# Two sets of transposes moved later, the pooling maps spread over four gate products, and a quarter of the weight splits given to ScalarE and VectorE

## The chip, the cores and the metric

The kernel runs on one core of one Trainium2 chip. The metric is the time on the device in microseconds (us), from launch to end; smaller is better. The kernel before has a median of 3289.72 us over three runs (3289.57 to 3299.82 us).

Engines in the text: TensorE (PE) multiplies, VectorE (DVE), ScalarE (ACT) and GpSimd (POOL) work on tiles in SBUF, PE writes into banks of PSUM, and SyncE (SP) and ACT issue most DMAs. Each engine executes its instructions in program order, so that an instruction that waits holds up all that stands behind it on its engine.

## The reference, cut to what matters

One layer of a streaming encoder on 2048 tokens of 1024 channels, all in float32. The part that the change touches is the input projection and what hangs on it:

```
proj = x @ w_in
q, c_kv, q_idx, w_idx, k_idx, pool_in, gate_logits = split(proj)
q     = rope(q)                                  # 8 heads of 128, first quarter rotated
k_lat = rope(c_kv);  k_idx = rope(k_idx);  q_idx = rope(q_idx)
attn  = sparse_indexed_attention(q, k_lat, c_kv, q_idx, w_idx, k_idx)   # top 256 keys of each query
pooled = trailing_mean(pool_in, windows 2/4/8/16) - pool_in
branch_b = (pooled @ w_pool per channel group * pool_scale) @ w_pool_branch
gate_a, gate_b = split(sigmoid(gate_logits))
mixed = (gate_a * branch_a + gate_b * branch_b) @ w_out
```

After it come two layer norms and a gated FFN with a short convolution, which the change leaves alone.

## The kernel before, in words

**Number format.** Products must keep float32 accuracy. Each operand is split into a high part, rounded to the matmul's input type, and the rest (`split`, line 312); each product is three matmuls (hi x hi, hi x lo, lo x hi; `mm3`). A product in the text, unless said otherwise, is 24 matmuls of 128x512 with a [128, 512] bank of PSUM as its sum. The split of a weight tile (128x1024) costs two operations in one of two ways: on POOL, in pieces of 256 columns (four pairs of TENSOR_SCALAR for the high part and TENSOR_TENSOR for the rest, printed as "x2" where two follow each other), or on ACT (an ACTIVATE for the high part) and DVE (a TENSOR_TENSOR for the rest). While the flag `self.shared` is set, which is until attention begins, weights asked for with `pool=True` go to POOL. Weights that are used by all four groups of tokens are split once, in group 0, written to DRAM and reloaded by the later groups.

**Stages.** The index projection comes first, for the four groups of 512 tokens. Then, for each group g: `proj_pool` (line 690, two weight chunks; in chunk 0 the two sums grow side by side in steps of one pair of channel blocks, so that i counts the steps in the loop of `run` at line 1866), `proj_q` (four chunks of 24 matmuls of 128x256 for each of four row blocks) and `proj_gates` (line 767). The latter has a first loop over j = 0 to 3 with two gate-a products each, here called p1 to p8, and a second loop with two gate-b products and two products of the pooling branch each. Attention follows (from about 1095 us), then the output projection and the FFN.

**Transposes.** Rotated keys and rotated query rows are [token, channel] and have to be turned by PE (128x128 transposes against `ident`). `keys` (line 631) does it for a group's keys, eight transposes into two banks that ACT and DVE copy out. For the last group, g = 3, it is the closure `done`, called at step i == 1 of `proj_pool(0)`. `store_q` (line 676) turns one chunk of query rows: twice four transposes, each followed by an ACT copy into an M buffer (a pool of eight) and a DMA from ACT's queue. `proj_q` keeps two chunks back; they are turned in `proj_gates` at j = 0 and j = 1.

**Pooling maps.** `pool_map` (line 752) multiplies each of the four pooled groups (p<-b,wpool, three matmuls each) and scales the result with ACT and DVE into two parts. It runs all four in a row at the start of j == 3, that is between p6 and p7.

**Banks.** `p1` has four one-bank tiles, given out in turn: a product can start when the tile handed out four requests earlier has been read. The sigmoid that reads a gate product is issued DG = 2 turns after the product.

**The background.** The sparse attention's top-k search for the first groups' queries runs in the background (`self.bg`, from `turn`): for each bit of a threshold, ACT counts with Sign (ACTIVATE m<-b,F) and DVE with TENSOR_SCALAR_CACHE_REDUCE (m<-b,F), and three small DVE operations decide (g, h, F). A step is put in when a model of the engines' clocks allows it, so its instructions stand in ACT's and DVE's program order between those of the projections.

Of the kernel before, what the change touches and what calls it, by code (L numbers as in the profile page):

```python
# [9 lines left out]
F32 = mybir.dt.float32  # L10
F32R = mybir.dt.float32r
# [3 lines left out]
AF = mybir.ActivationFunctionType  # L15
OP = mybir.AluOpType
# [3 lines left out]
P = 128  # L20
NB = S // P
G = 512
# [71 lines left out]
            1: ((0, 0, OP.add), (1, 1, OP.add)), 3: ((0, 1, OP.add), (1, 1, OP.add)), 6: ((1, 1, OP.add),),  # L94
            5: ((0, 1, OP.add), (0, 0, OP.subtract)), 7: ((0, 0, OP.add),)}
LASTK = 6
SCAN = 1.04
PIECE = 256

# [20 lines left out]
class Paced:  # L120
# [5 lines left out]
    def __getattr__(self, name):  # L126
# [4 lines left out]
        def call(*args, **kw):  # L131
# [4 lines left out]
            else:  # L136
# [10 lines left out]
                if name == "tensor_tensor_scan":  # L147
                    rate = SCAN
                now = max(getattr(self._c, self._w), self._c.pe)
# [110 lines left out]
class Kern:  # L260
    def __init__(self, ctx, tc, a, out):
        self.clocks = Clocks()
        self.tc, self.nc, self.a, self.out = tc, PacedCore(tc.nc, self.clocks), a, out
        self.stores, self.older, self.bg, self.late = [], [], [], []
        self.const = ctx.enter_context(tc.tile_pool(name="const", bufs=1))
        self.big = ctx.enter_context(tc.tile_pool(name="big", bufs=42))
        self.mid = ctx.enter_context(tc.tile_pool(name="mid", bufs=8))
        self.sm = ctx.enter_context(tc.tile_pool(name="sm", bufs=4))
        self.early_pool = tc.alloc_tile_pool(name="early", bufs=1)
        self.late_pool = None  # L270
        self.p1 = ctx.enter_context(tc.tile_pool(name="p1", bufs=4, space=PSUM))
        self.p2 = ctx.enter_context(tc.tile_pool(name="p2", bufs=2, space=PSUM))
        self.dram = ctx.enter_context(tc.tile_pool(name="dram", bufs=1, space=bass.MemoryType.DRAM))
        self.n, self.shared = 0, True
        self.credit = self.seen = 0.0

    def _name(self, s):
# [34 lines left out]
    def split(self, hi, lo, src, pool=False):  # L312

        nc = self.nc
        if pool:
            m = PIECE if self.shared else src.shape[1]  # L320
            if self.shared and len(src.shape) == 3:
                k = src.shape[2]
                m = max(1, PIECE // k)
            for i in range(0, src.shape[1], m):
                c = slice(i, i + m)
                nc.gpsimd.tensor_scalar(hi[:, c], src[:, c], 1.0, 1.0, op0=OP.mult, op1=OP.mult)
                nc.gpsimd.tensor_tensor(lo[:, c], src[:, c], hi[:, c].bitcast(F32), op=OP.subtract)
        else:
            nc.scalar.activation(hi, src, AF.Copy)
            nc.vector.tensor_tensor(lo, src, hi.bitcast(F32), op=OP.subtract)  # L330
# [418 lines left out]
        if self.lazy:  # L749
            self.lazy.pop(0)()  # L750

    def pool_map(self, g):
        nc = self.nc
        self.pm = []
        for k in range(4):
            t = self.pooled[k]
            ps = self.PS1()
            self.mm3(ps, self.wpool[:, 0, k], self.wpool[:, 1, k], t[:, 0], t[:, 1], True, True)
            o = self.T([P, 2, G], F32R)
            sc = self.pscale[:, k:k + 1]  # L760
            nc.scalar.activation(o[:, 0], ps, AF.Identity, scale=sc)
            nc.vector.scalar_tensor_tensor(o[:, 1], ps, sc, o[:, 0].bitcast(F32), op0=OP.mult, op1=OP.subtract)
            self.pm.append(o)
            yield 0.7

    def proj_gates(self, g):
        nc = self.nc
        base = g * self.nab + 6
        for j in range(4):
            w = self.ab.get(base + j)  # L770
            if j == 3:
                yield from self.pool_map(g)
            if self.qpend and j < 2:
                self.store_q()
            while self.lazy or j and self.fins:
                self.lazy_step()
            for i in range(2):
                ps = self.PS1()
                yield from self.proj_t(ps, w, i * P)

                def gate(dst=self.d_gm[g][:, 2 * j + i, 0], ps=ps):
                    ga = self.M([P, G])
                    nc.scalar.activation(ga, ps, AF.Sigmoid)
                    nc.scalar.dma_start(dst, ga)

                self.after(DG, gate)
                yield 5.2
        for j in range(4):
            w = self.ab.get(base + 4 + 2 * j)
            if j == 2:  # L790
                if g + 1 < NG:
                    self.load_parts(g + 1, range(NPRE))
                else:
                    self.attn_load()
            if j == 3 and g + 1 == NG:
                self.attn_setup()
                self.load_q(0)
                self.attention_start()
            gates = []
            for i in range(2):  # L800
                ps = self.PS1()
                yield from self.proj_t(ps, w, i * P)

                def gate(ps=ps):
                    gb = self.M([P, G])
                    nc.scalar.activation(gb, ps, AF.Sigmoid)
                    gates.append(gb)

                self.after(DG, gate)
                yield 5.2  # L810
            if j == 3 and g + 1 < NG:
                self.load_parts(g + 1, range(NPRE, DC // 2))
            if j == 3 and g + 1 == NG:
                self.scores_to(1)
            (wh, wl), = self.ab.get(base + 5 + 2 * j)
            for i in range(2):
                ps = self.PS1()
                c0 = i * P
                for k in range(4):
                    self.mm3(ps, wh[:, k, c0:c0 + P], wl[:, k, c0:c0 + P], self.pm[k][:, 0], self.pm[k][:, 1],  # L820
                             k == 0, k == 3)
                    if k in FW:
                        yield FINE
                self.flush()
                nc.vector.tensor_tensor(gates[i], ps, gates[i], op=OP.mult)
                self.store(self.d_gm[g][:, 2 * j + i, 1], gates[i])
                if j == 3 and g + 1 == NG:
                    self.scores_to(2 * i + 2)
                yield 2.6
# [851 lines left out]
    def down_half(self, hf):  # L1681
# [34 lines left out]
        for mi, m in enumerate(DOWN):  # L1716
# [5 lines left out]
            final = hf == 1 and mi == len(DOWN) - 1  # L1722
            lastk = LASTK if final else 2 if hf == 0 and mi == 4 else 3 if hf == 0 and mi == 5 else 0
            held = []
# [114 lines left out]
    def run(self):  # L1839
        self.qpend, self.rows, self.wi_parts, self.keyed, self.selected = [], {}, [], -1, 1  # L1840
        self.early, self.xr, self.xraw = {}, {}, {}
        self.qraw, self.qs, self.unit, self.avq, self.tails = {}, {}, {}, [], []
        self.pair, self.spill = {}, []
        self.load_x(0, range(1))
        self.posi = self.M([NB, P], I32)
        self.nc.sync.dma_start(self.posi, self.a["positions"].rearrange("o (b p) -> (o b) p", p=P))
        self.psc = self.M([4, P])
        self.nc.sync.dma_start(self.psc, self.a["pool_scale"].rearrange("o (g p) -> (o g) p", p=P))
        self.setup()
        self.wi.raw[0] = [self.wi.load_one(0, 0)]  # L1850
        self.load_x(0, range(1, 2))
        self.wi.raw[0].append(self.wi.load_one(0, 1))
        self.load_x(0, range(2, DC // 2))
        self.split_ahead(0, 1)
        self.wi.split(0)
        self.split_ahead(0, 1)
        for groups in GROUPS:
            self.bg.append((lambda g=groups[-1]: self.keyed >= g, self.scores_and_selection(groups)))
        done = None
        for g in range(NG):  # L1860
            self.run_to_end(self.proj_index(g, done))
            while self.spill:
                self.store(*self.spill.pop(0))
            done = self.finish_index(g)
        self.load_parts(0, range(NFIRST, DC // 2))
        for g in range(NG):
            for i, step in enumerate(self.proj_pool(g)):
                if i == 1 and g == 0:
                    done()
                    self.wi_parts = None  # L1870
                self.turn(step)
            self.run_to_end(self.proj_q(g))
            self.run_to_end(self.proj_gates(g))
        self.shared = False
        self.run_to_end(self.attention())
        self.settle()
        self.run_to_end(self.mix_out())
        self.settle()
        self.run_to_end(self.ffn())
        self.settle()  # L1880
        self.late_pool.release()
# [30 lines left out]
```

## Time and profile before

| | us |
|---|---|
| median of three runs | 3289.72 |
| the profiled execution | 3292.94 |
| its span, first to last instruction | 3291.2 |
| mean granted TensorE clock | 0.982 of full speed |
| PE busy | 3157.8 (96%) |
| DVE / ACT / POOL busy | 2417.7 / 1559.4 / 1279.9 |
| PE busy between 195 and 360 us | 131.5 of 165 |
| PE busy between 360 and 437 us | 75.6 of 77 |
| PE busy between 437 and 1095 us | 648.9 of 658 |

A row of the timeline gives the start, the duration, the engine, the operation, the tiles (output <- inputs, with buffer numbers left out), how often it follows itself, and in brackets the idle time ahead of it with what ended it. Nearly all operations are recorded under line 153, the wrapper that issues them, so they are told apart by tiles and shapes. A row of the windows gives the busy time of each engine in a stretch (with the count of instructions), the granted TensorE clock, the DMA share and GB/s. PE's busy rows in the stage from 195 to 360 us are the projections of group 0.

### The profile page before, as it was taken

What the parts mean: (1) busy time and instruction counts of PE and PEld (TensorE: products, weight loads), DVE (VectorE), ACT (ScalarE), POOL (GpSimd) and SP (SyncE); (2) the same over time, 40 slices, a digit from 0 to 9 for tenths busy, and PEclk for the clock granted to TensorE, in tenths of its full rate; (3) what the DMA queues carried; (4) which work ended last, traced back from release to release, by engine and by line L of the source; (5) the groups of instructions that cost most, each with busy time, mean ns of one, the idle gap of its engine ahead of it and who ended that gap; (6) DMA issues with size and microseconds to landing.
All of it is one profiled execution on the core that took longest, in us unless ns stands there. A gap on an engine that the chain in (4) does not pass through costs nothing. (4 is left out here: it accounts for less than half of the span.)

```text
span 3291.2 us, 46503 instructions
## 1 busy us (share of the span) xinstructions
PE 3157.8 (96%) x15918; PEld 2654.2 (81%) x15918; DVE 2417.7 (73%) x4271; ACT 1559.4 (47%) x2656; POOL 1279.9 (39%) x1314
## 2 busy tenths in 40 slices
PE   8988899999999899999999999999999999999998
PEld 8877688898898788788878877777778778888787
DVE  5588859986988777777766666666688865555797
ACT  3466537846777466666621133333343433222443
POOL 3139411020010688766641143443166511121673
PEclk9999899999999899999999999999999999999999
DMA  8457565653665444434464459899797665566984
GB/s 327 148 199 275 191 251 195 246 203 136 227 226 194 144 172 172 157 130 161 157 224 147 156 186 320 309 327 339 288 380 264 208 252 224 224 238 246 364 296 163
DMA packets 325675, 745.68 MB, mean 227 GB/s; under 512 B 30074, under 2 KB 115006, under 8 KB 325438
## 3 DMA queue, kind: packets, MB, share of 16 engines
q1 hardware_dynamic: 315646, 724.88, 61.5%
q10 hardware_dynamic: 9792, 17.83, 1.4%
q8 instruction: 126, 2.06, 0.3%
q14 instruction: 111, 0.91, 0.1%
HBM read 514.36 MB, written 228.23 MB: 226 GB/s over the span
## 5 line engine op out<-in xcount | busy, mean ns | idle before, releaser
L153 PE MATMUL p<-b,b 128*128 128x512 f32 (+3 forms) x12644 | 2783.7, 369 | 56.1 <-ACT b L153 24.4
L153 PEld LDWEIGHTS p<-b,b 128*128 128x128 f32 x12644 | 2175.7, 191 | 453.0 <-ACT b L153 25.0
L153 ACT ACTIVATE b<-p 128x512 fp32r<-128x512 f32 (+9 forms) x726 | 427.7, 612 | 653.6 <-PE p L153 627.0
L153 ACT ACTIVATE b<-b 128x1024 fp32r<-128x1024 f32 (+2 forms) x248 | 253.6, 1028 | 390.7 <-POOL b L153 136.4
L153 DVE TENSOR_TENSOR b<-b,b 128x1024 fp32r<-128x1024 f32 (+6 forms) x246 | 369.6, 1541 | 42.6 <-ACT b L153 39.8
L153 ACT ACTIVATE m<-b,F 128x1024 bf16<-128x1024 f32 (+3 forms) x352 | 345.8, 985 | 68.0 <-DVE F L153 43.8
L153 DVE TENSOR_SCALAR_CACHE_REDUCE m<-b,F 128x768 bf16<-128x768 f32 (+4 forms) x374 | 346.8, 949 | 11.8 <-DMA q<-m 9.9
L153 POOL TENSOR_TENSOR b<-b,b 128x256 fp32r<-128x256 f32 (+3 forms) x276 | 314.1, 1152 | 101.7 <-ACT b L153 84.9
L153 DVE TENSOR_TENSOR m<-m,p 128x512 f32<-128x512 f32 x176 | 120.3, 684 | 242.8 <-ACT b L153 182.6
L153 POOL TENSOR_TENSOR m<-b,b 128x512 f32<-128x512 f32 x99 | 140.2, 1425 | 337.4 <-issue 258.6
L153 DVE SCALAR_TENSOR_TENSOR b<-b,cw,b 128x1023 f32<-128x1023 f32 (+1 forms) x176 | 245.0, 1392 | 26.2 <-ACT b L153 25.1
L153 DVE TENSOR_TENSOR b<-p,b 128x512 fp32r<-128x512 f32 (+1 forms) x286 | 201.7, 714 | 72.3 <-ACT b L153 69.7
L153 POOL TENSOR_SCALAR b<-b 128x256 fp32r<-128x256 f32 (+3 forms) x216 | 125.8, 596 | 325.6 <-DMA b<-in_w_in_dram 122.8
L153 PE MATMUL p<-b 128*128 128x512 f32 x616 | 235.1, 393 | 5.8 <-ACT b L153 4.0
L153 POOL TENSOR_TENSOR b<-b,m 128x512 f32<-128x512 f32 x110 | 192.0, 1760 | 123.8 <-DMA m<-in_w_ffn_down_dram 74.0
L153 PE MATMUL p<-ident,b 128*128 128x128 f32 x1456 | 213.1, 274 | 24.8 <-ACT b L153 13.5
L153 DVE CUSTOM_DVE_ANT_0 b<-p,b 128x1024 f32<-128x1024 f32 (+7 forms) x192 | 174.2, 909 | 65.8 <-PE p L153 64.5
L153 PEld LDWEIGHTS p<-ident,b 128*128 128x128 f32 x1456 | 174.2, 141 | 58.7 <-ACT b L153 16.5
L153 ACT ACTIVATE b<-b,mx 128x1024 f32<-128x1024 f32 (+7 forms) x192 | 171.5, 896 | 69.7 <-DVE mx L153 63.7
L153 ACT ACTIVATE m<-p 128x512 f32<-128x512 f32 (+1 forms) x180 | 104.9, 594 | 193.6 <-PE p L153 178.9
L153 DVE SCALAR_TENSOR_TENSOR b<-b,ws,b 128x768 f32<-128x768 f32 (+5 forms) x154 | 159.8, 1065 | 40.6 <-ACT b L153 38.6
L153 PE MATMUL p<-kst,b 128*128 128x384 f32 (+3 forms) x656 | 150.6, 359 | 4.1 <-ACT b L153 2.6
(130 smaller groups left out, 2360.8 us busy)
## 6 DMA issues: line engine op xcount, KB each, us to landing
b<-uw SPq DMA_DIRECT2D x308, 512.0 KB, 6.5
b<-wp SPq DMA_DIRECT2D x192, 512.0 KB, 5.8
uw<-l SPq DMA_DIRECT2D x98, 512.0 KB, 3.0
b<-in_w_ffn_down_dram SPq DMA_DIRECT2D x154, 256.0 KB, 5.3
b<-h SPq DMA_DIRECT2D x154, 256.0 KB, 5.3
wp<-b SPq DMA_DIRECT2D x64, 512.0 KB, 5.2
uw<-b SPq DMA_DIRECT2D x56, 512.0 KB, 3.5
h<-m SPq DMA_DIRECT2D x110, 256.0 KB, 5.9
```

The lines of the kernel that those rows point to most:

```text
L153: return f(*args, **kw)
```

## The change

Four edits:

1. `done`, the key transposes of the last group, is called at step 5 instead of step 1 of `proj_pool(0)`, after the sums of chunk 0 instead of between their parts.
2. The two chunks of query rows that are left over are turned at j = 1 and 2 of the gates instead of j = 0 and 1, in all four groups.
3. `pool_map` makes one map a call. The maps come after the products p4, p5, p6 and p7 instead of all four between p6 and p7. Each of these products now yields twice (2.6 and 2.6) instead of once (5.2), and the four yields of the old `pool_map` are gone, so the number of turns is the same. The same lines in the second loop never apply, as 9 + 2j + i is over 7.
4. `split` counts its calls; while `self.shared` is set, every fourth call that asks for POOL goes to ACT and DVE instead.

```diff
 LASTK = 6
+KEYS_AT = 5
+PM_AT = (4, 5, 6, 7)
...
     def split(self, hi, lo, src, pool=False):
         nc = self.nc
-        if pool:
+        self.turns += 1
+        if pool and (not self.shared or self.turns % 4):
             m = PIECE if self.shared else src.shape[1]
...
-    def pool_map(self, g):
+    def pool_map(self, k):
         nc = self.nc
-        self.pm = []
-        for k in range(4):
-            t = self.pooled[k]
-            ...
-            self.pm.append(o)
-            yield 0.7
+        t = self.pooled[k]
+        ...
+        self.pm.append(o)
...
     def proj_gates(self, g):
+        self.pm = []
         for j in range(4):
             w = self.ab.get(base + j)
-            if j == 3:
-                yield from self.pool_map(g)
-            if self.qpend and j < 2:
+            if self.qpend and 1 <= j < 3:
                 self.store_q()
...
                 self.after(DG, gate)
-                yield 5.2
+                if 2 * j + i + 1 in PM_AT:
+                    yield 2.6
+                    self.pool_map(len(self.pm))
+                yield 2.6
...
             for i, step in enumerate(self.proj_pool(g)):
-                if i == 1 and g == 0:
+                if i == KEYS_AT and g == 0:
                     done()
```

In the order of the instructions it looks so. On PE in `proj_pool(0)` before, the eight key transposes (out of the two M tiles that the rope fills) stand between two steps of chunk 0's sums p_699 and p_700:

```order
L153 MATMUL p_700_2898<-b_2854,b_2190 128x512
L153 MATMUL p_700_2898<-b_2853,b_2191 128x512
L153 MATMUL p_701_2923<-ident_84,m_2763 128x128
L153 MATMUL p_702_2924<-ident_84,m_2764 128x128
...
L153 MATMUL p_699_2897<-b_2857,b_2200 128x512
L153 MATMUL p_699_2897<-b_2858,b_2200 128x512
```

After, at the same place of PE's program, they stand behind the end of both sums, ahead of chunk 1's first product p_736:

```order
L155 MATMUL p_700_2886<-b_2856,b_2200 128x512
L155 MATMUL p_700_2886<-b_2855,b_2201 128x512
L155 MATMUL p_722_2991<-ident_84,m_2757 128x128
L155 MATMUL p_723_2992<-ident_84,m_2758 128x128
...
L155 MATMUL p_736_3036<-b_2204,b_2867 128x512
L155 MATMUL p_736_3036<-b_2205,b_2867 128x512
```

The 24 matmuls that close the two sums have moved ahead of the transposes; the next product's weight b_2867 and b_2868 is one of those that ACT and DVE split now.

On PE in the gates of group 0 before, p6 ends (p_1140), the four maps follow, and p7 (p_1184) begins:

```order
L153 MATMUL p_1140_4540<-b_2861,b_4299 128x512
L153 MATMUL p_1168_4631<-b_3338,wpool_586 128x512 x3
L153 MATMUL p_1171_4641<-b_3516,wpool_586 128x512 x3
L153 MATMUL p_1178_4662<-b_3745,wpool_586 128x512 x3
L153 MATMUL p_1180_4669<-b_4032,wpool_586 128x512 x3
L153 MATMUL p_1184_4681<-b_2210,b_4459 128x512
```

After, p4 ends (p_1086), and the first map, the second left-over chunk's two sets of transposes and p5 (p_1127) follow; the other maps stand behind p5, p6 and p7:

```order
L155 MATMUL p_1086_4334<-b_2855,b_4091 128x512
L155 MATMUL p_1105_4399<-b_3320,wpool_586 128x512 x3
L155 MATMUL p_1123_4441<-ident_84,b_3870 128x128 x4
L155 MATMUL p_1125_4449<-ident_84,b_3870 128x128 x4
L155 MATMUL p_1127_4457<-b_2204,b_4237 128x512
```

With four banks in turn, p5's bank is that of p4, so p5 now stands behind p4's sigmoid. Before, four requests ahead of p5 lay a transposed set of query rows.

On ACT in the same group after, among the gate-b products, the high part b_5112 of a gate-b weight is made between Sign counts and the followers of the search's end (tn is its threshold); before, POOL made it:

```order
L155 ACTIVATE m_5020,wa_2711<-b_2419,F_4977 128x896
L155 ACTIVATE b_5075<-b_2282,tn_5064 128x768
L155 ACTIVATE m_5058<-p_1294_4997 128x512
L155 ACTIVATE b_5112<-b_4979 128x1024
L155 ACTIVATE b_5144<-b_2573,tn_5064 128x1024
```

On DVE the rest, b_5113, stands behind what follows that threshold (the masks b_5076 and b_5077, with the scan as SCALAR_TENSOR_TENSOR b<-b):

```order
L155 TENSOR_SCALAR tn_5064<-t_5063 128x2
L155 TENSOR_SCALAR b_5076<-b_5075 128x768
L155 SCALAR_TENSOR_TENSOR b_5077<-b_5076 128x768
...
L155 TENSOR_TENSOR b_5075<-b_5075,b_5076 128x768
L155 TENSOR_SCALAR b_5108<-b_5075 128x768
L155 TENSOR_TENSOR b_5113<-b_4979,b_5112 128x1024
```

So this weight is now made in the order of the search. In all, eleven tiles change over: POOL's order has 1079 rows instead of 1123, DVE's and ACT's have eleven more each. One is a weight of `proj_pool` ahead of the stage, eight lie in group 0, and two (the value up-projection and one query tile) at the start of attention.

More of the change, by code (lines that the diff above doesn't have):

```diff
@@ L273, in __init__ @@
         self.dram = ctx.enter_context(tc.tile_pool(name="dram", bufs=1, space=bass.MemoryType.DRAM))
-        self.n, self.shared = 0, True
+        self.n, self.shared, self.turns = 0, True, 0
         self.credit = self.seen = 0.0
@@ L750, in lazy_step @@
             self.lazy.pop(0)()
-    def pool_map(self, g):
+    def pool_map(self, k):
         nc = self.nc
-        self.pm = []
-        for k in range(4):
-            t = self.pooled[k]
[L757 to L762, printed above, removed]
-            self.pm.append(o)
-            yield 0.7
+        t = self.pooled[k]
+        ps = self.PS1()
+        self.mm3(ps, self.wpool[:, 0, k], self.wpool[:, 1, k], t[:, 0], t[:, 1], True, True)
+        o = self.T([P, 2, G], F32R)
+        sc = self.pscale[:, k:k + 1]
+        nc.scalar.activation(o[:, 0], ps, AF.Identity, scale=sc)
+        nc.vector.scalar_tensor_tensor(o[:, 1], ps, sc, o[:, 0].bitcast(F32), op0=OP.mult, op1=OP.subtract)
+        self.pm.append(o)
     def proj_gates(self, g):
@@ L809, in proj_gates @@
                 self.after(DG, gate)
-                yield 5.2
+                if 9 + 2 * j + i in PM_AT:
+                    yield 2.6
+                    self.pool_map(len(self.pm))
+                yield 2.6
             if j == 3 and g + 1 < NG:
```

## The prediction

> **What bounds the kernel now.** I read the busy times of a few stretches first, then PE's waits in the one stretch where PE is not full, and then the timelines there. Columns of the first row: length, busy time of PE, its weight loads, DVE, ACT and POOL, then the clock.
>
> ```profile
> 195.00:360.00 165.00, 131.51 (x723) 113.44 (x722) 150.33 (x409) 105.84 (x215) 118.81 (x216) 0.87 0.72 252
> PE p L153 <- ACT m L153: 10.6, 4, 5.1
> PE p L153 <- DVE m L153: 10.2, 6, 4.0
> PE p L153 <- ACT b L153: 9.3, 4, 3.5
> PE p L153 <- DVE b L153: 3.4, 1, 3.4
> ```
>
> PE lacks 33.5 us here, and the four rows (total, times, longest) add up to that. Elsewhere PE leads; only here, where DVE is busy 150 of 165 us, can an edit to order pay. The places:
>
> ```profile
> 208.75 0.48 PE L153 MATMUL p<-ident,m 128*128 128x128 f32 x1 [3.98 <-DVE m L153]
> ...
> 214.91 47.26 PE L153 MATMUL p<-b,b 128*128 128x512 f32 x312
> ...
> 310.39 22.05 PE L153 MATMUL p<-b,b 128*128 128x512 f32 x96 [0.74 <-ACT m L153]
> 332.27 0.87 PE L153 MATMUL p<-b,wpool 128*128 128x512 f32 x3
> ...
> 345.60 1.65 PE L153 MATMUL p<-b,wpool 128*128 128x512 f32 x3 [5.13 <-ACT m L153]
> 350.62 9.70 PE L153 MATMUL p<-b,b 128*128 128x512 f32 x33 [3.38 <-DVE b L153]
> 359.71 74.73 PE L153 MATMUL p<-b,b 128*128 128x512 f32 x329
> ```
>
> The keys' transposes (p<-ident,m) wait 10.2 us for the rope's last copies on DVE. The maps wait for sigmoids on ACT, and p7 for the first map's eviction on DVE. A warm matmul is 74.73 / 329 = 0.227 us, a product of 24 is 5.45. From p6's end at 332.27 to p7 at 350.62 are 18.35 us, of which four maps at full clock are 12 x 0.227 = 2.7; so 15.6 us are lost, and more behind them, because the clock falls:
>
> ```profile
> 345.00:350.00 5.00, 1.65 (x3) 0.83 (x3) 4.83 (x9) 1.86 (x5) 3.80 (x7) 0.50 0.53 150
> 350.00:355.00 5.00, 4.38 (x11) 3.50 (x12) 4.93 (x14) 3.48 (x8) 0.00 (x0) 0.52 1.02 396
> ```
>
> With a clock of 0.52 until 355, p7's first 4.4 us do half their work: 4.38 x 0.48 = 2.1 us lost.
>
> What do ACT and DVE hold? ACT stands about 12 us behind PE: p4 is the second product of the row at 310.39 and ends near 310.39 + 10.9 = 321.3, its sigmoid runs here:
>
> ```profile
> 333.72 0.57 ACT L153 ACTIVATE m<-p 128x512 f32<-128x512 f32 x1
> ...
> 324.09 5.29 DVE L153 SCALAR_TENSOR_TENSOR g<-wd,wa 128x4 f32<-128x4 f32 x1
> ...
> 332.30 0.16 DVE L153 SCALAR_TENSOR_TENSOR g<-wd,wa 128x4 f32<-128x4 f32 x1
> ...
> 345.27 3.56 DVE L153 SCALAR_TENSOR_TENSOR g<-wd,wa 128x4 f32<-128x4 f32 x1
> ```
>
> The lag is the search's: ACT's counts wait for DVE's decisions, and the same four-column decision takes 0.16 us or, beside POOL, 3.56 and 5.29.
>
> **What POOL costs DVE, and what a tile moved is worth.** The four commonest decisions from 195 to 360 us, POOL's split pieces there, and the split on DVE and ACT before 195 us, where it has no POOL beside it for the most part:
>
> ```profile
> L153 DVE SCALAR_TENSOR_TENSOR g<-wd,wa 128x4 f32<-128x4 f32 x26 | 15.7, 605 | 4.6 <-ACT m L153 3.9
> L153 DVE TENSOR_SCALAR h<-g 128x4 int32<-128x4 f32 x26 | 9.8, 378 | 0.8
> L153 DVE TENSOR_SCALAR h<-g 128x2 int32<-128x2 f32 x27 | 9.4, 347 | 0.9
> L153 DVE SCALAR_TENSOR_TENSOR g<-wd,wa 128x2 f32<-128x2 f32 x27 | 8.9, 330 | 0.4
> ...
> L153 POOL TENSOR_TENSOR b<-b,b 128x256 fp32r<-128x256 f32 x96 | 70.4, 755 | 0.0
> L153 POOL TENSOR_SCALAR b<-b 128x256 fp32r<-128x256 f32 x94 | 38.1, 423 | 6.7 <-DMA b<-in_w_in_dram 6.7
> ...
> L153 DVE TENSOR_TENSOR b<-b,b 128x1024 fp32r<-128x1024 f32 x17 | 20.8, 1243 | 12.8 <-ACT b L153 12.3 <-DMA xT<-b 0.3
> ...
> L153 ACT ACTIVATE b<-b 128x1024 fp32r<-128x1024 f32 x17 | 17.5, 1053 | 8.8 <-DMA b<-in_xT_dram 6.6 <-DMA b<-in_w_in_dram 2.2
> ...
> L153 DVE TENSOR_TENSOR b<-b,b 128x1024 fp32r<-128x1024 f32 x142 | 238.5, 1719 | 36.3 <-ACT b L153 34.5 <-DMA x<-b 0.9 <-DMA xT<-b 0.3
> ```
>
> 96 pieces are 24 tiles, (70.4 + 38.1) / 24 = 4.5 us of POOL each. The 106 decisions take 43.8 us where 106 x 0.16 would be 17.0: 26.8 us extra, or 1.1 us of DVE a tile. The rope's and other small operations suffer too, so I put a removed tile at 1.1 to 2.0 us of DVE. On the bill stand 1.24 us on DVE (1.72 if the mean of the whole kernel holds, the last row) and 1.05 us on ACT. The net for DVE lies between +0.6 and -0.8 us; I take -0.4, nearer the relief, since the operations counted are only part of those that suffer. Four such tiles lie ahead of p4's sigmoid: -1.6 us.
>
> The Trainium skill, "SBUF — State Buffer", on the port pair that DVE and GpSimd share, speaks against this edit: a DVE operation with two SBUF inputs, and the split's rest is one, and a GpSimd operation that reads SBUF lock each other out for a whole instruction. By it the moved split would be held up by one POOL piece, about 0.7 us, and each tile would end near -0.4 + 0.7 = +0.3 us, +1.2 in place of -1.6. The trace agrees in direction but not in the length of the hold: 5.29 us is seven pieces.
>
> **Keys' transposes.** They come 24 matmuls later, 5.45 us of PE. The end of the rope is the condition:
>
> ```profile
> 205.47 0.76 DVE L153 TENSOR_TENSOR rope<-b,sin 128x72 f32<-128x72 f32 x1
> ...
> 213.83 0.23 DVE L153 TENSOR_TENSOR rope<-b,sin 128x72 f32<-128x72 f32 x1
> ...
> 214.50 0.23 DVE L153 COPY m<-b 128x128 f32<-128x128 f32 x1
> ...
> 211.09 1.40 POOL L153 TENSOR_TENSOR b<-b,b 128x256 fp32r<-128x256 f32 x2
> ```
>
> The last copy ends at 214.73. PE would be at the transposes near 202 + 5.45 = 207.5, so they still wait, 3 to 10 us. Rope operations take 0.76 beside POOL and 0.23 once POOL stops at 212.5. In the new order two of POOL's tiles stand behind the copies of chunk 0's sums and wait for them, which frees the rope; three or four us of search that DVE did later now stand inside the rope. I put the last copy at 211 to 218. PE then has 24 matmuls done that it did not have, a head start of 4 to 7 us on PE. It doesn't reach the end by itself: DVE gets on only as far as its own work shrinks. I count 3 us on DVE (some 12 rope operations at 0.5 us less, less half of that for POOL's tiles that now run beside the search); from 0 to 5.
>
> **Query rows.** The first set of gate transposes at j = 0 goes. Its copies filled the M buffers, and ACT waited for their DMA:
>
> ```profile
> 302.11 1.04 ACT L153 ACTIVATE m<-b,F 128x896 bf16<-128x896 f32 x1 [2.44 <-DMA q<-m]
> ```
>
> That is ahead of p4's sigmoid; the set that comes at j = 2 instead is behind it. I count half, 1.2 us (0 to 2.4). The DMAs leave ACT's queue later, and attention reads them some 700 us on: nothing.
>
> **Maps.** p5 takes p4's bank, so p5 begins where p4's sigmoid ends: at 333.72 + 0.57 = 334.3 with the old lag. The first map and the two sets of transposes come ahead in PE's time, at no cost. So the stall of 15.6 us shrinks but does not go: the new one is at p5. From it p5, two maps and p6 are 2 x 5.45 + 2 x 0.68 = 12.3 us, plus 2 us for the cold clock behind the stall; p7 would begin at 348.6. Before, p7 began at 350.62 and lost 2.1 more: 352.7. So the new order alone is worth 4.1 us, and each us by which the sigmoid comes earlier counts in full. That is 1.6 + 3 + 1.2 = 5.8 us by the terms above; the decision that was held for 5.29 us may be held or not. Gain at p7: about 10 us (4 to 18).
>
> **What is late next.** Behind p7 PE was full (74.73 us in one row). The gate-b weight b_5113 was made by POOL, and is now made by DVE behind the threshold's scan:
>
> ```profile
> 387.92 1.43 POOL L153 TENSOR_TENSOR b<-b,b 128x256 fp32r<-128x256 f32 x2
> ...
> 393.66 0.92 DVE L153 TENSOR_SCALAR b<-b 128x768 bf16<-128x768 f16 x2
> ```
>
> POOL was done at 389.3. The product that uses it was 157 matmuls into PE's long row, at 359.71 + 157 x 0.227 = 395.4. DVE reaches its new place at 394.5 less the 5.8 us by which DVE is ahead, 388.7, and ends at 389.9; PE, 10 us ahead, asks at 385.4. That takes back 4.5 us (0 to 8); 5.5 are left.
>
> **Groups 1 to 3** have no stall at the maps:
>
> ```profile
> 572.05 22.03 PE L153 MATMUL p<-b,b 128*128 128x512 f32 x96
> 593.92 3.08 PE L153 MATMUL p<-b,wpool 128*128 128x512 f32 x12
> ...
> 344.39 0.67 ACT L153 ACTIVATE b<-p,pscale 128x512 fp32r<-128x512 f32 x1
> ```
>
> Now the map's eviction on ACT (0.67) and p4's sigmoid (0.57) must be over before p5, while PE has eight transposes, about 1 us, to do. With half a us for hand-overs p5 waits 0.7, three times: 2.1 us lost; with a Sign of 1.1 us and more ahead of them, 3 each, or 9.
>
> **Attention's start**, where two more tiles move:
>
> ```profile
> 1099.80 3.78 PE L153 MATMUL p<-b,b 128*128 128x128 f32 x10 [4.16 <-ACT b L153]
> 1105.13 12.39 PE L153 MATMUL p<-b,b 128*128 128x128 f32 x43 [1.55 <-DVE b L153]
> ```
>
> These 5.7 us may shrink, since POOL stands less beside the last threshold, or grow, since DVE makes a query tile's rest behind a scan: 1 us gained, between 3 and -3.
>
> **The sum**: 10 - 4.5 - 2.1 + 1 = 4.4 us. The profiled execution of 3292.94 would become 3288.5; against the median, which is 3.2 lower, 3289.7 - 4.4 = 3285.3. I say 3285.
>
> **The rivals.** About 0.3% of the time, 9.9 us, is what a measurement of this kernel can tell from no change.
>
> *The forecast*: DVE and ACT still hold group 0, most of the gain is given back at p5 and at the late weight. 3285, by itself 3279 to 3293. Chance 0.45.
>
> *POOL was the whole lag.* If the two long holds of 5.29 and 3.56 us go, 8.5 us come on top of the 5.8: p7 gains about 18, the late weight is no later than DVE, which is 14 ahead (4 us given back), and 18 - 4 - 2 + 1 = 13; with a rope that ends in time for the keys up to 20. 3270 to 3277. For it: the two rows. Against: what starts a hold is chance, and POOL is still busy for four fifths of the time. Chance 0.33.
>
> *ACT and DVE take over POOL's waits, and it gets slower.* POOL waited for its raw tile 6.7 us (the row with in_w_in_dram). Should such a tile now stand in ACT's program, the Sign counts and sigmoids behind it wait too, and p5 to p8 with them. Price: 6.7 us less 2 of PE's lead, the 4.5 us at the late weight doubled, 9, and 3 us in each later group: 4.7 + 9 + 9 - 10 = +13, 3303. It decides from the point at which the lag behind PE at p5 is as large as before, above 12 us. Against: the tile with that wait is used far behind p7, and ACT gets to it later than its landing at 336. By the skill's lock (above) DVE's terms lose 2.8 us; that alone gives 3288. Chance 0.15.
>
> *The change does nothing that counts*: the keys wait just as long, the stall at p5 is the stall at the maps. 3290, within the bound. Chance 0.07.
>
> **How the numbers follow.** Faster by over 9.9 us: the second case, and a tenth of the first: 0.37. Slower: the third, less its milder part: 0.14. Within: 0.49. The range goes from the second case's 3268 to the third's milder part, 3297; left out are the far end of the third, and gains over 22 us.
>
> **What would show it.** Right: the keys' transposes still wait, 3 us or more, behind 24 more matmuls; the four waits of the maps are gone, and one wait of 5 to 10 us stands ahead of p5, ended by ACT's sigmoid; p7 starts near 342; a wait for DVE b of 3 to 5 us near 385 in the long row; in the later groups a wait under 1 us ahead of p5; POOL has 44 rows less. Wrong: p5 starts without a wait (the second case), or a wait in the Signs that a DMA into b ends (the third).

## The result, and the profile after

The changed kernel takes 3260.86 us (median of four runs, 3258.85 to 3268.61) against 3293.33 of the kernel before in the same series (3289.57 to 3299.82): a ratio of 0.9904, with a 95% interval of 0.9878 to 0.9929, or 32 us less. The forecast was 3285 in a range of 3268 to 3297. The direction was right, the size was out of the range. The profiled execution of the changed kernel took 3268.61 us with a span of 3266.8. It is the longest of the four, so the two traces are only 24.4 us apart and show three quarters of the 32.

The stretch of group 0 in the changed kernel, in the columns used before, and PE's waits in it:

```profile
195.00:360.00 165.00, 148.99 (x816) 129.80 (x816) 153.86 (x464) 125.81 (x250) 95.68 (x170) 0.94 0.73 254
PE p L155 <- ACT b L155: 8.5, 6, 3.9
PE p L155 <- ACT m L155: 3.7, 1, 3.7
PE p L155 <- POOL b L155: 3.0, 1, 3.0
PE p L155 <- DVE m L155: 0.9, 1, 0.9
```

PE's waits fell from 33.5 us to 16.1. POOL is busy 95.7 us instead of 118.8, ACT 125.8 instead of 105.8. On PE's timeline the places of the prediction are these:

```profile
208.60 0.33 PE L155 MATMUL p<-ident,m 128*128 128x128 f32 x1 [0.87 <-DVE m L155]
211.63 45.62 PE L155 MATMUL p<-b,b 128*128 128x512 f32 x312 [2.70 <-ACT b L155]
...
298.22 12.78 PE L155 MATMUL p<-b,b 128*128 128x512 f32 x48 [3.68 <-ACT m L155]
...
315.53 7.33 PE L155 MATMUL p<-b,b 128*128 128x512 f32 x24 [2.95 <-POOL b L155]
...
329.57 5.62 PE L155 MATMUL p<-b,b 128*128 128x512 f32 x24
...
376.13 37.96 PE L155 MATMUL p<-b,b 128*128 128x512 f32 x166 [1.68 <-DVE b L155]
```

The keys' last transpose waits 0.87 us. p5 starts at 315.53 after a wait of 2.95 us, and the profile puts that down to its weight from POOL. p7 starts at 329.57 where it started at 350.62, and forecast was 342. The late weight b_5113 costs 1.68 us. The sigmoid of p4 runs here on ACT:

```profile
314.80 0.58 ACT L155 ACTIVATE m<-p 128x512 f32<-128x512 f32 x1
```

It ends at 315.38, only 0.15 us ahead of p5, whose bank is p4's: without POOL's weight, the sigmoid would have held p5 nearly as long. p4 ends at 298.22 + 12.78 = 311.0, so ACT's lag is 3.8 us; it was 12. Why it fell so far is what the experiments are about.

For the whole program I use two points that all kernels pass with the same work behind them: M1, the row of 96 matmuls of 128x256 in group 1's query projection, and M2, the first row of twelve 128x512 matmuls in attention. For M2, before and after:

```profile
1127.84 2.68 PE L153 MATMUL p<-b,b 128*128 128x512 f32 x12
```

```profile
1101.64 2.69 PE L155 MATMUL p<-b,b 128*128 128x512 f32 x12
```

M1 comes 19.8 us earlier (524.64 against 544.47), M2 26.2. So some 20 us are won in group 0 and 6 more between group 1 and attention's start. From M2 to the end of the span these two traces are alike, 2163.4 and 2165.2 us. There is one trace of each kernel, though, and over all the kernels below this rest lies between 2155.5 and 2166.5 us, with nothing changed in it.

### The profile page after: what moved, and what is told of

The parts are those of the page before. It is cut to its first block, busy times and chain, and to the rows that moved or that the text cites. A ratio compares the mean times of both kernels' runs of the same rounds, so it can differ in the third digit from the quotient of the medians.

```text
span 3266.8 us, 46425 instructions
## 1 busy us (share of the span) xinstructions
PE 3153.3 (97%) x15918; PEld 2654.1 (81%) x15918; DVE 2409.1 (74%) x4282; ACT 1568.0 (48%) x2667; POOL 1217.7 (37%) x1226
## 5 line engine op out<-in xcount | busy, mean ns | idle before, releaser
L155 ACT ACTIVATE b<-b 128x1024 fp32r<-128x1024 f32 (+2 forms) x259 | 264.8, 1028 | 393.1 <-POOL b L155 130.9
L155 DVE TENSOR_TENSOR b<-b,b 128x1024 fp32r<-128x1024 f32 (+4 forms) x257 | 386.1, 1539 | 41.7 <-ACT b L155 39.5
L155 POOL TENSOR_TENSOR b<-b,b 128x256 fp32r<-128x256 f32 (+3 forms) x232 | 284.5, 1239 | 103.8 <-ACT b L155 87.1
L155 DVE SCALAR_TENSOR_TENSOR b<-b,cw,b 128x1023 f32<-128x1023 f32 (+1 forms) x176 | 244.1, 1387 | 26.2 <-ACT b L155 25.1
L155 POOL TENSOR_SCALAR b<-b 128x256 fp32r<-128x256 f32 (+3 forms) x172 | 97.0, 576 | 367.1 <-DMA b<-in_w_in_dram 147.0
```

What stands on the lines that cost most here:

```text
L155: return f(*args, **kw)
```

## The experiments

The first theory, A, is that the order counts: the rope runs beside an idle POOL, and the maps meet sigmoids that are there. The rival, B, is that the moved splits count. Each of the first kernels holds one part or leaves one out. Times are the ratio to the kernel before with its 95% interval; of the traces, M1 and M2 against the kernel before.

| kernel | ratio | interval | M1, us | M2, us |
|---|---|---|---|---|
| changed kernel | 0.9904 | 0.9878 to 0.9929 | -19.8 | -26.2 |
| keys only | 0.9975 | 0.9964 to 0.9986 | -3.9 | -4.5 |
| maps and rows only | 0.9978 | 0.9965 to 0.9991 | +3.4 | -1.6 |
| splits only | 0.9936 | 0.9923 to 0.9949 | -19.1 | -18.2 |
| all but the splits | 0.9951 | 0.9939 to 0.9963 | -9.5 | -6.6 |
| all but the keys | 0.9932 | 0.9920 to 0.9944 | -14.8 | -14.9 |
| all but maps and rows | 0.9930 | 0.9917 to 0.9944 | -24.7 | -26.6 |

**Keys only.**

```diff
-                if i == 1 and g == 0:
+                if i == 5 and g == 0:
                     done()
```

> The kernel before with the keys' transposes at step 5 alone. Theory A (order: the rope runs beside an idle GpSimd and gives its time to the search's decisions): the four-column decisions come 8 to 12 us earlier from 206 us on, and the time falls by 6 to 10 us. Theory B (the splits that leave GpSimd are what counts): the decisions come at most 3 us earlier, and the time falls by less than 3 us.

At first the search's decisions come earlier as A has it, and the time falls by 8 us (0.25%). Here are the first four-column decision and the two around 315 us; before, they stood at 218.60, 316.96 and 329.62:

```profile
208.84 0.15 DVE L153 TENSOR_SCALAR F<-h 128x4 int32<-128x4 int32 x1
...
312.56 0.32 DVE L153 SCALAR_TENSOR_TENSOR F<-h,F 128x4 int32<-128x4 int32 x1
327.37 0.16 DVE L153 SCALAR_TENSOR_TENSOR F<-h,F 128x4 int32<-128x4 int32 x1
```

A lead of 9.8 us is 4.4 at 312.56 and 2.3 behind it: between the two decisions lie 14.8 us. One operation takes most of them, and it ends when POOL's pieces end; these are rows of DVE and POOL:

```profile
318.36 8.77 DVE L153 SCALAR_TENSOR_TENSOR g<-wd,wa 128x4 f32<-128x4 f32 x1
...
333.55 0.77 POOL L153 TENSOR_SCALAR b<-b 128x256 fp32r<-128x256 f32 x2 [6.44 <-DMA b<-in_w_in_dram]
```

POOL stops at 333.55 - 6.44 = 327.11, the decision ends at 327.13. In the kernel before it is the same: the held decision of the prediction ends at 324.09 + 5.29 = 329.38, and POOL stops at 336.09 - 6.72 = 329.37:

```profile
336.09 0.77 POOL L153 TENSOR_SCALAR b<-b 128x256 fp32r<-128x256 f32 x2 [6.72 <-DMA b<-in_w_in_dram]
```

**Maps and rows only.** The changed `proj_gates` and `pool_map`, with KEYS_AT = 1 and the old condition in `split`.

> The kernel before with the query rows and the maps moved, keys and splits as before. Theory A: the four waits at the maps become one at p5, some 10 us shorter in sum, and the time falls by 8 to 14 us. Theory B: the sigmoids stay as late as they were, p5 waits 10 us, and the time falls by at most 4 us.

7 us less in all, which lies between the two theories, but 3.4 us more in group 0: there B is right. p5 waits as the prediction said it would:

```profile
324.17 8.36 PE L155 MATMUL p<-b,b 128*128 128x512 f32 x24 [11.90 <-ACT m L155]
...
309.54 12.49 DVE L155 SCALAR_TENSOR_TENSOR g<-wd,wa 128x4 f32<-128x4 f32 x1
```

The 11.9 us at p5 come of a decision that is held for 12.5 us. By the prediction's terms with no shift it would be 11.3: 334.3, less p4's end at 321.3, a map of 0.7 and transposes of 1. What is won comes later in the program.

**Splits only.**

```diff
-        if pool:
+        self.turns += 1
+        if pool and (not self.shared or self.turns % 4):
```

> The kernel before with every fourth split given to ScalarE and VectorE, nothing moved. Theory A: the decisions of the search come 0 to 3 us earlier, the time falls by 0 to 5 us, most of it at the start of attention. Theory B: they come 8 us earlier or more, and the time falls by 10 to 20 us.

The counter takes in every call of `split`; of the 39 weight tiles that POOL splits in pieces of 256 columns, eleven move. 21 us less, just over B's range. But B's way isn't it either: the decisions are not 8 us earlier all along. The lead is 2.0 us at the decision that stood at 316.96 before, and 11.4 at the next:

```profile
314.92 0.16 DVE L153 SCALAR_TENSOR_TENSOR F<-h,F 128x4 int32<-128x4 int32 x1
318.20 0.16 DVE L153 SCALAR_TENSOR_TENSOR F<-h,F 128x4 int32<-128x4 int32 x1
```

3.3 us lie between them, 12.7 before. The gain comes in one jump, where a decision was held. The hold is not the whole jump, though. In the kernel before, the step from one decision to the next also holds a wait:

```profile
316.96 0.32 DVE L153 SCALAR_TENSOR_TENSOR F<-h,F 128x4 int32<-128x4 int32 x1
...
322.48 0.75 DVE L153 TENSOR_SCALAR_CACHE_REDUCE m<-b,F 128x512 bf16<-128x512 f32 x1 [2.53 <-DMA q<-m]
...
329.62 0.16 DVE L153 SCALAR_TENSOR_TENSOR F<-h,F 128x4 int32<-128x4 int32 x1
```

Of the 9.4 us by which the step is shorter, 5.1 are the hold (5.29 against 0.16) and 2.5 this wait for the DMA of the query rows; ACT waits 3.44 us for it in the same place. With the splits moved, the hold and both waits are gone, though the rows stand where they stood. The DMA engines' share between 300 and 330 us is 0.98 before and 0.75 here. How the moved splits shorten that wait is not tested by any run. The second hold of the kernel before, 3.56 us at 345.27, makes another: its two decisions (340.41 and 349.06) were 8.7 us apart and are 3.3 apart here. No operation of the search is held over 2 us in this kernel.

**All but the splits.** The changed kernel with the old condition in `split`.

> The changed kernel with all splits back on GpSimd. Theory A: it keeps 20 to 28 us of the gain of about 31. Theory B: it keeps 5 to 15.

16 us less, so neither number, closer to B. p5 waits 11.07 us, and a decision takes 5.96 us; its end at 323.27 is again POOL's:

```profile
317.31 5.96 DVE L155 SCALAR_TENSOR_TENSOR g<-wd,wa 128x4 f32<-128x4 f32 x1
...
337.67 0.77 POOL L155 TENSOR_SCALAR b<-b 128x256 fp32r<-128x256 f32 x2 [14.42 <-DMA b<-in_w_pool_branch_dram]
```

337.67 - 14.42 = 323.25. So a new theory, C: where POOL runs piece upon piece without a pause, a small operation of DVE can be held until the run ends, and the moved tiles cut the run. The rival, D, is that only the sum of POOL's work beside DVE counts.

**All but the keys**, KEYS_AT = 1 in the changed kernel.

> The changed kernel with the keys' transposes back at step 1, splits and maps as changed. If the parts add up (8 us for the keys alone, 7 for the maps alone, 21 for the splits alone, 32 for all): 3 to 8 us slower than the changed kernel. If the keys' gain is swallowed once the splits have moved: within 2 us of it.

0.9932 against 0.9904, or 9 us slower: the parts add up within the measurement, with intervals that overlap. In the traces the keys are worth 5 us at M1 (-14.8 against -19.8) and 11 at M2.

**All but maps and rows.** The kernel before with the new `split` and the keys at step 5.

> The changed kernel with the maps and the query rows back where they were. If the maps are worth what they are alone: 3 to 8 us slower than the changed kernel. If the stall at the maps is only the search's lag, and the moved splits have taken that away: within 2 us of it.

The medians give the maps and rows some 8 us, with intervals that overlap; the traces give them nothing at M2 (-26.6 against -26.2), and a loss of 5 us in group 0, which is won back by then. But the trace of the changed kernel is of its longest execution, and this one of the shortest of five. So what the maps' edit is worth beside the other two stays open within 0 to 8 us.

**POOL reads the moved tiles too.** To put POOL's load back without undoing the move:

```diff
         else:
+            if pool:
+                flat = src if len(src.shape) == 2 else src.rearrange("p a b -> p (a b)")
+                for i in range(9):
+                    s = flat[:, i * 112:(i + 1) * 112]
+                    n = s.shape[1]
+                    nc.gpsimd.tensor_scalar(self.dum[:, :n], s, 1.0, 1.0, op0=OP.mult, op1=OP.mult)
+                    nc.gpsimd.tensor_tensor(self.dum[:, :n], s, self.dum[:, :n], op=OP.subtract)
             nc.scalar.activation(hi, src, AF.Copy)
```

> The changed kernel, with GpSimd reading each moved tile as well, in nine pairs of 112-column operations whose results nobody uses. Theory C (GpSimd's unbroken run of pieces holds a two-input decision of VectorE until the run ends; the moved tiles break the run): holds of 4 us or more between 300 and 350 us come back, p5 waits 8 us or more for ScalarE, and 10 to 18 of the 32 us are given back. Theory D (it is the sum of VectorE's small savings, the order of the splits, or the earlier release of buffers): no long hold, at most 6 us given back.

0.9983 (0.9974 to 0.9993): 26 of the 32 us are given back, more than C said, and without the hold that C said. This kernel tells them apart badly. It is 10 us behind at the first decision (216.25 against 206.08), since PE waits ahead of the stretch, too, and later ACT waits for POOL's pooling sums, which stand behind the added reads:

```profile
165.68 1.97 PE L155 MATMUL p<-ident,b 128*128 128x128 f32 x8 [4.44 <-ACT b L155]
...
254.08 0.63 ACT L155 ACTIVATE b<-m 128x512 fp32r<-128x512 f32 x1 [9.35 <-POOL m L155]
```

On the hold alone it says more. POOL is busy for 28.1 of the 30 us from 300 to 330, where it was 29.4 before and 8.7 in the changed kernel, and nothing is held. So the sum of POOL's work does not make a hold. Nor does this kernel speak against C, for the added pieces let DVE in. There are gaps of some 0.1 us between them, and the decisions' operations beside them are short:

```profile
319.80 0.42 POOL L155 TENSOR_TENSOR dum<-b,dum 128x112 f32<-128x112 f32 x1
320.28 0.17 DVE L155 TENSOR_SCALAR h<-g 128x4 int32<-128x4 f32 x1
320.31 0.28 POOL L155 TENSOR_SCALAR dum<-b 128x112 f32<-128x112 f32 x1
...
325.87 0.80 POOL L155 TENSOR_SCALAR b<-b 128x256 fp32r<-128x256 f32 x2
325.98 0.35 DVE L155 TENSOR_SCALAR h<-g 128x4 int32<-128x4 f32 x1
```

Beside the added pieces from 291 to 299 and from 316 to 324 us, 21 of these operations take 0.20 us each, 0.29 at most. Beside split pieces from 301 to 316 and from 324 to 337 us, 27 of them take 0.39 on average. What limits C is the changed kernel itself, where POOL runs piece upon piece from 281.25 to 308.74 - 8.57 = 300.17 and nothing is held:

```profile
281.25 0.22 POOL L155 TENSOR_TENSOR m<-head,b 128x16 f32<-128x16 f32 x1 [6.70 <-DVE m L155]
...
308.74 0.77 POOL L155 TENSOR_SCALAR b<-b 128x256 fp32r<-128x256 f32 x2 [8.57 <-DMA b<-in_w_in_dram]
```

So a run of 19 us, with one split of DVE's in it that stretched a pair of POOL's pieces to 2.40 us, need not bring a hold.

**POOL waits at every second tile.** The kernel before, with a copy of DVE's latest decision on POOL ahead of every second weight tile.

> The kernel before, with GpSimd waiting for VectorE's latest decision ahead of every second weight tile in group 0; no split is moved. Theory C: no decision takes over 2 us between 300 and 350 us, the sigmoid of p4 comes 5 us earlier or more, and the time falls by 3 to 15 us unless a weight comes late. Theory D: the long holds stay, or go without any gain; the time is the same or up to 10 us longer.

0.9976 (0.9965 to 0.9987), 8 us less, but the trace has a hold of 12.18 us, this time of a one-input operation. No copy stood inside the run of POOL from 292 to 328:

```profile
315.50 12.18 DVE L153 TENSOR_SCALAR h<-g 128x4 int32<-128x4 f32 x1
...
335.44 0.19 POOL L153 COPY seen<-gaps 128x1 int32<-128x1 int32 x1 [7.78 <-DVE gaps L153]
```

335.44 - 7.78 = 327.66, the end of the hold is 327.68. The run was not cut, so the theory was not tested; the same end was seen again. The traced execution, 3291.15 us, is the longest of twelve, and its M2 is no earlier than before; whether the shorter ones have the hold isn't known.

**POOL bound to DVE at every tile.** Now the tie is in the data: the first piece of each tile takes its factor, 1.0, from a column that DVE makes from the latest decision.

```diff
+                one = 1.0
+                if self.shared and i == 0 and self.last is not None:
+                    self.turns += 1
+                    one = self.gaps[:, self.turns % 16:][:, :1]
+                    nc.vector.tensor_scalar(one, self.last[:, :1], 0.0, 1.0, op0=OP.mult, op1=OP.add)
-                nc.gpsimd.tensor_scalar(hi[:, c], src[:, c], 1.0, 1.0, op0=OP.mult, op1=OP.mult)
+                nc.gpsimd.tensor_scalar(hi[:, c], src[:, c], one, 1.0, op0=OP.mult, op1=OP.mult)
```

> The kernel before, with the first piece of every weight tile that GpSimd splits in group 0 taking its factor 1.0 from VectorE, which makes it from the search's latest decision; so GpSimd can't run more than two tiles (9 us) ahead of VectorE, and no split is moved. Theory C (GpSimd's unbroken run holds a decision until it ends): no decision between 300 and 350 us takes over 9 us, the longest step between two four-column decisions falls from 13 us to 9 or less, and the time falls by 5 to 15 us unless weights come late. Theory D (the sum of GpSimd's work beside VectorE counts, not how it is cut up): the time is within 5 us of the kernel before, or longer.

0.9963 (0.9950 to 0.9977): 12 us less than the kernel before, with no split moved, nothing reordered and POOL made to wait. POOL's run from 290 to 329 is now in pieces:

```profile
307.17 0.48 POOL L153 TENSOR_SCALAR b<-b,gaps 128x256 fp32r<-128x256 f32 x1 [5.62 <-DVE gaps L153]
323.56 0.48 POOL L153 TENSOR_SCALAR b<-b,gaps 128x256 fp32r<-128x256 f32 x1 [7.61 <-DVE gaps L153]
334.25 0.48 POOL L153 TENSOR_SCALAR b<-b,gaps 128x256 fp32r<-128x256 f32 x1 [1.90 <-DVE gaps L153]
```

The two decisions that had 12.7 us between them have 6.7, and no operation of a decision between 300 and 350 us takes over 1.1 us:

```profile
312.76 0.33 DVE L153 SCALAR_TENSOR_TENSOR F<-h,F 128x4 int32<-128x4 int32 x1
319.49 0.16 DVE L153 SCALAR_TENSOR_TENSOR F<-h,F 128x4 int32<-128x4 int32 x1
```

The hold is gone and the time is in C's range (5 to 15). Two things keep this from being proof. In the trace p7 starts 10.7 us earlier, but M1 is only 5.1 us earlier and M2 5.7; the other 6.5 us lie behind M2, where nothing is tied. And the tie also moves POOL's work away: POOL is busy for 16.8 us between 300 and 330, 29.4 before. So C is well supported for the hold, as the kernel of the added reads has POOL's work there without the hold. How much of the time it is worth is open, and so is where the other 9 us of the splits' 21 come from: POOL's smaller load, D's way, and the shorter wait for the rows' DMA are both only argued.

**Every third split, every second split.** `self.turns % 3` and `self.turns % 2` in the changed kernel.

> The changed kernel with every third split of GpSimd's moved instead of every fourth. Theory C: the holds were gone already, so nothing more is to be had: within 3 us of the changed kernel, or slower by up to 8 as each tile costs VectorE 1.2 us. Theory D: 3 to 6 us faster than the changed kernel.

> The changed kernel with every second split moved. Theory C: 0 to 12 us slower than the changed kernel. Theory D: 5 to 15 us faster.

0.9948 (0.9935 to 0.9962) and 0.9940 (0.9925 to 0.9956), both some 12 to 15 us slower than the changed kernel, as C had it for the second and more than it had for the first; the second interval overlaps the changed kernel's. Neither is faster, as D had it. With every third tile the keys' transposes end later (chunk 1 starts at 217.58, not 211.63) and the late weight is later:

```profile
217.58 47.69 PE L155 MATMUL p<-b,b 128*128 128x512 f32 x336 [2.79 <-ACT b L155]
...
384.05 47.11 PE L155 MATMUL p<-b,b 128*128 128x512 f32 x197 [4.98 <-DVE b L155]
```

That is the late weight of the prediction, close to the 4.5 us it gave. For every second tile the profiled span, 3262.2, is shorter than the changed kernel's while the median is longer; the execution that was profiled, 3264.39 us, is the shortest of the six by 10 us. I take the medians.

**Query rows early.** `if self.qpend and j < 2` in the changed kernel.

> The changed kernel with the two chunks of query rows turned at j = 0 and 1 again. If the rows' copies and their DMAs hold ScalarE ahead of p4's sigmoid, as the prediction counts: 1 to 3 us slower. If it is the place of the maps alone that counts: within 1 us.

0.9896 (0.9879 to 0.9912): no difference to the changed kernel that these runs can tell, where 1.2 us were counted. In group 0 the move even costs time. With the rows early, p5's bank isn't p4's; p5 doesn't wait, and p7 starts at 325.09 instead of 329.57. M1 comes 6.6 us earlier than in the changed kernel, M2 at the same place (1101.86 against 1101.64). Four kernels (this one, the changed one, all but maps and rows, every second split) have M1 between 518.1 and 526.0 and M2 within 0.8 us of each other: something at attention's start takes up what is won beyond that, and no run tests what. No kernel was faster than the changed one beyond the intervals.

## Why the prediction was wrong

- **The step that failed** is the one on the tiles moved: "Four such tiles lie ahead of p4's sigmoid: -1.6 us", with the sentence that the decision "that was held for 5.29 us may be held or not", and the rival's "what starts a hold is chance". The splits alone measured 21 us (0.64%). In one trace of each kernel the holds are not strewn by chance: in all five kernels in which POOL's splits are whole and its run is not cut (before, keys only, maps only, all but the splits, waits at every second tile) an operation of DVE was held for 5.3 to 12.5 us between 309 and 329 us; in the eight with moved splits and the one with a tie at every tile, none over 2.3 us up to 360. The rows were quoted; I priced them at a mean of 1.1 to 2.0 us a tile, and a mean over tiles has no term for an operation that waits for the last tile of a run of nine (290 to 329 us, 4.4 us each). What picks the operation stays open: ahead of the held one, the decisions' operations passed in the same run in at most 0.7 us. "POOL is still busy for four fifths of the time", which spoke against the rival, doesn't fit the rows either: it was busy for 72% of the stretch before and 58% after.
- **What followed from it.** p4's sigmoid came 18.9 us earlier (314.80 against 333.72), not 5.8. At the decision ahead of the hold's place the search was 11.0 us early (305.99 against 316.96), the keys' term with it, and at the next 20.1 (309.57 against 329.62): there lie the hold and the wait for the rows' DMA, which no term priced at this place. So p5 waited 2.95 us, and p7 gained 21 us, not 10; the range of 4 to 18 left it out. The rival "POOL was the whole lag" had the two rows and 18 us at p7, and came closest; its end of 3270 to 3277 was still 9 us short.
- **Keys.** The mechanism was right, the size was not: the rope, beside an idle POOL, ran ahead. The last copy ended at 208.5, not 211 to 218, and the transposes waited 0.87 us, not 3 to 10. The first decision came 12.5 us earlier, then 8; 3 were counted. Alone, much of it was lost in group 0 to a longer hold, 8.77 us: M1 came 3.9 us earlier.
- **Maps.** The stall at p5 was rightly seen: 11.9 and 11.07 us in the two kernels without moved splits, 11.3 without shift by the prediction's terms. "So the new order alone is worth 4.1 us" was wrong for group 0, where it lost 3.4 us at M1.
- **The late weight** b_5113 was late as said, by 1.68 us, not 4.5: DVE was ahead, too, by more than counted. It was 4.98 us late with every third tile moved.
- **Groups 1 to 3.** 0.45 us ahead of p5 in group 1, 0.39 in group 3 and no such wait in group 2, against 0.7 each. Between M1 and M2 the changed kernel won 6 us, where -2.1 + 1 was counted. What won them stays open: maps only won 5.0 there, but all but the splits, with the same maps, lost 2.9.
- **The port's rule.** The Trainium skill, "SBUF — State Buffer", section "Who interferes with whom", on the pair of ports that DVE and GpSimd share, says that one holds it for a whole instruction. The end of each hold fits: it is GpSimd's. Its length doesn't: 12.49 us are more than twenty of POOL's pieces, and the prediction's 5.29 us are about ten, not seven. The +0.7 us a tile was charged to the wrong engine. Of the six splits on DVE in the stretch five took 1.21 to 1.41 us, and one 1.83 (at 345.07, POOL's last pieces beside its first 0.75 us). Where the split started first, it was POOL that waited: its pair of pieces took 2.47 us instead of 1.43 in these rows of the kernel with the splits only:

```profile
232.40 1.23 DVE L153 TENSOR_TENSOR b<-b,b 128x1024 fp32r<-128x1024 f32 x1
232.46 2.47 POOL L153 TENSOR_TENSOR b<-b,b 128x256 fp32r<-128x256 f32 x2
```

## What to carry to other kernels

When a short operation takes 0.2 to 0.7 us a hundred times and 5.29 us once, don't average: find what ended at the same moment, and ask what makes that run so long. An engine that is busy for 72% of a stretch can still hold another by working without a pause at the wrong time, and then a cut in its run, by a tie in the data or by a few tiles given to other engines, can be worth more than the work it moves.

## What the runs showed of the hardware

A hold hits operations with one input as well as with two (12.18 us for TENSOR_SCALAR h<-g). In four of the five kernels its end was that of POOL's run to 0.02 us. With maps only it came 0.6 us ahead of that, 0.1 us behind the last TENSOR_TENSOR of the run, with two TENSOR_SCALAR pieces still to come. The later, shorter holds of the kernels before, keys only, maps only and waits at every second tile (3.55 to 5.62 us) end with POOL's run to 0.03 us as well. DVE's counts over 128x768 in the same stretch took 1.00 us throughout, and were never held.
